# Rotary angles computed inside the first MLP, and the gMLP's v in 512-column products

## The chip, the cores and the metric

The kernel runs on one NeuronCore of one Trainium2 chip. The metric is the device time of one execution in microseconds (us), lower is better. Five engines run side by side, each with an instruction stream of its own: TensorE (PE; its weight loads are listed as PEld), VectorE (DVE), ScalarE (ACT), GpSimd (POOL) and SyncE (SP), which here issues the DMAs. An engine starts its instructions in the order of its stream; an instruction that waits holds up all that stands behind it on that engine.

## The reference

Two transformer blocks follow each other on 256 rows of 1024 columns, all in float32. The part around the change is this, cut down:

```python
# gMLP (layer 0 of the second block), GATE_DIM = 2048
z = gelu(hn @ w_in);  u, v = split(z, 2)
v = layernorm(v, ln_g, ln_b)
sv = einsum('gij,bnjgc->bnigc', masked w_s, v in blocks) + b_s
h = h + (u * sv) @ w_out
# MLP 0
h = h + square(relu(rmsnorm(h) @ w1)) @ w2
# shared latent keys and values, then attention (layer 1)
inv_freq = 10000 ** (-arange(0, 64, 2) / 64)
ang = positions[:, None] * inv_freq
c, s = cos(ang), sin(ang)          # used by apply_rope on k_pe and q_pe
```

The angles hang on the positions alone, so their sine and cosine can be made at any time before the latents.

## The kernel before, in words

**Products.** Every float32 matrix product is made in three passes: an operand is split into a high part and the rest (names ending in `h` and `l`), and `mm3` issues high times high, high times rest, rest times high. `fm` keeps the weights stationary and moves 256 columns of the activations (PE rows that read `xTh,s1h`: moving `xT`, stationary `s1`); `tm` keeps the activations stationary and moves the weights' columns (rows that read `s4h,xTh`), for one half `t` of the rows (128 of 256) at a time. `down` is `tm` with 512 columns. Every matmul has a weight load of its own.

**Weights.** All weights come as a fixed sequence of chunks (`weight_plan`), 1 MB each in two halves of 512 KB. SP loads a half into one of four `raw` buffers; ACT writes the high part of it into a slot (`s0h`, `s1h`, ...), DVE the rest (`s0l`, ...); the buffer is then loaded again. Slots are reused as soon as the chunk in them has been used up.

**Order.** The order on each engine is not written out. The kernel's parts are generators that offer one instruction at a time, and `run_threads` picks the one that an estimate of the engines' times starts first; waits such as `self.on(...)` act in that planner only. So an edit moves instructions elsewhere too.

**Stages.** Token mixer, conv FFN, gMLP, MLP 0, latents, attention, MLP 1. Between two stages stands a junction: residual, mean square on ACT, `rstd` on DVE and POOL (a power of -0.5), scaling (`r_xg`) on DVE, four transposes per 512 columns on PE, then `xTh` on ACT and `xTl` on DVE. It runs for the rows of t = 0 first; while t = 1 is in its junction, PE makes the first chunks' products for t = 0 alone ("stagger"; 4 chunks in the gMLP, `STAGV`, 3 in the MLPs, `STAG`), with `tm` and 256 columns, copied out into `tmst` and transposed. After that come `up` (w1, one chunk: 48 matmuls of 256 columns) and `down` (w2, one chunk: 24 matmuls of 512 columns) in turn; `down` i follows `up` i + 4 (`LAG`).

**gMLP v.** `v_part` multiplies one chunk of w_in (1024 rows by 256 columns, 8 row blocks) with `tm`: 24 matmuls of 256 columns for each t, 16 such products. `v_out` applies Gelu (ACT) and, after every second chunk, takes statistics of 512 columns (DVE). `layernorm` begins when all are through; the first matmul on v (`sv`) waits for it.

**Angles.** `latent_setup` runs at the start of MLP 0 and spawns `angles` with priority 8. `angles` first issues the load of `inv_freq` on SP (broadcast to 128 partitions, into a corner of `vm[0]`), converts the positions (`vm<-c_pos`), multiplies by `inv_freq`, reduces the argument and ends in two Sin activations that write `cs`. All DVE work of it writes `vm`. `cs` is first read in the latents.

Of the kernel before, what the change touches and what calls it, by code (L numbers as in the profile page):

```python
# [13 lines left out]
AF = mybir.ActivationFunctionType  # L14
# [8 lines left out]
STAG, STAGF, STAGV = 3, 4, 4  # L23
# [174 lines left out]
class Kernel:  # L198
# [611 lines left out]
    def gmlp(self, pool):  # L810
        S, V, T, G = self.S, self.V, self.T, self.G
        wsT = self.load(pool, "wsT")

        def mask_ws():
            yield self.on(("a_v", 1))
            yield from G.memset(wsT[64:, :, :64], 0.0)

        self.spawn(1, mask_ws())
        bs = self.tile(pool, [P, 8, P], "bs")
        self.bcast(bs.rearrange("p g i -> p (g i)"), "b_s")  # L820
        lng = self.bcast(self.tile(pool, [P, 2048], "lng"), "ln_g")
        lnb = self.bcast(self.tile(pool, [P, 2048], "lnb"), "ln_b")
        v = [self.tile(pool, [P, 2048], f"v{t}") for t in range(2)]
        hT = self.hT
        st = [self.tile(self.pers, [P, 4, 6], "bst", bufs=2) for t in range(2)]
        vs = []

        def v_part(w, c, t):
            o = (yield from self.bank("fm"))[:, :256]
            yield from self.tm(o, w.view(8), hT, t, range(8), ev="a_v")  # L830
            vs.append(self.spawn(1, v_out(o, c, t)))

        def v_out(o, c, t):
            yield from S.activation(v[t][:, c * 256:(c + 1) * 256], o, AF.Gelu)
            self.rel(o)
            if c % 2:
                yield from V.bn_stats(st[t][:, c // 2, :], v[t][:, (c - 1) * 256:(c + 1) * 256])

        def layernorm(t):
            yield self.join(vs)  # L840
            mv = self.tile(self.scr, [P, 2], "mv", bufs=2)
            yield from V.bn_aggr(mv, st[t])
            r = yield from self.rstd(mv[:, 1:2], 1, 1.0)
            for h in range(4):
                s = slice(512 * h, 512 * (h + 1))
                yield from V.scalar_tensor_tensor(v[t][:, s], v[t][:, s], mv[:, 0:1], lng[:, s], op0=ALU.subtract, op1=ALU.mult)
                yield from V.scalar_tensor_tensor(v[t][:, s], v[t][:, s], r, lnb[:, s], op0=ALU.mult, op1=ALU.add)
            self.set(("ln", t), v[t])

        ws = []  # L850
        for t in range(2):
            for c in range(STAGV):
                if len(ws) <= c:
                    ws.append((yield from self.chunk("a_v", c)))
                yield from v_part(ws[c], c, t)
                if t:
                    self.free(ws[c])
        for c in range(STAGV, 8):
            w = yield from self.chunk("a_v", c)
            for t in range(2):  # L860
                yield from v_part(w, c, t)
            self.free(w)
        for t in range(2):
            self.spawn(1, layernorm(t))
        self.set(("a_u", 0))
        self.set(("a_u", 1))
        aT = {}

        def block(i, o):
            u = yield from self.take(pool, [P, 512], "u", o)  # L870
            yield from S.activation(u, o, AF.Gelu)
            self.rel(o)
            sv = yield from self.bank("tp", ev=[("ln", 0), ("ln", 1)])
            for b in range(2):
                for t in range(2):
                    c0 = i * 256 + b * P
                    yield from T.matmul(sv[:, (2 * b + t) * P:(2 * b + t + 1) * P], v[t][:, c0:c0 + P], wsT[:, i, :],
                             start=True, stop=True)
            w = yield from self.take(pool, [P, 512], "svb")
            yield from V.tensor_tensor(w.rearrange("p (a i) -> p a i", a=4), sv.rearrange("p (a i) -> p a i", a=4),  # L880
                            bs[:, i:i + 1, :].to_broadcast([P, 4, P]), op=ALU.add)
            self.rel(sv)
            yield from V.tensor_tensor(w, w, u, op=ALU.mult)
            self.rel(u)
            aT[i] = yield from self.take_aT(pool, i, LAG + 1)
            yield from self.split(aT[i][0].rearrange("p a b -> p (a b)"), aT[i][1].rearrange("p a b -> p (a b)"), w)
            self.rel(w)
            self.set(("a_u", "block", i), aT[i][1])

        yield from self.updown(("a_u", "a_w_out"), 8, 1, pool, block, aT,  # L890
                               lambda t, acc: self.next_norm(t, acc, [(self.g[0], "w1_0")]), 0, ("norm_mlp_g0",))
# [479 lines left out]
            self.set(("o", t, b), l)  # L1371


    def angles(self, pool, pi):

        S, V = self.S, self.V
        scratch = self.vm[0]
        fr = self.bcast(scratch[:, 128:160], "inv_freq")
        pf = scratch[:, 160:162]
        yield from V.tensor_copy(pf, pi)  # L1380
        cs = self.cs = self.tile(pool, [P, 2, 2, 32], "cs")
        a, n = scratch[:, 0:64], scratch[:, 64:128]
        for t in range(2):
            yield from V.tensor_scalar(a[:, 32 * t:32 * t + 32], fr, pf[:, t:t + 1], None, op0=ALU.mult)
        magic = 1.5 * 2.0 ** 23
        parts = (6.28125, 0.0019340515136718750, 1.2554228305816650390625e-06)
        rest = 2 * np.pi - sum(parts)
        for big in (4096.0, 1.0):
            yield from V.tensor_scalar(n, a, float(np.float32(1.0 / (2 * np.pi * big))), magic, op0=ALU.mult, op1=ALU.add)
            yield from V.tensor_scalar(n, n, -magic, None, op0=ALU.add)  # L1390
            for c in parts + (rest,):
                yield from V.scalar_tensor_tensor(a, n, -float(np.float32(c * big)), a, op0=ALU.mult, op1=ALU.add)
        pi_lo = float(np.nextafter(np.float32(np.pi), np.float32(0)))
        yield from V.tensor_scalar(n, a, np.pi / 2, None, op0=ALU.is_gt)
        yield from V.scalar_tensor_tensor(n, n, -2 * np.pi, a, op0=ALU.mult, op1=ALU.add)
        yield from V.tensor_scalar(n, n, np.pi / 2, pi_lo, op0=ALU.add, op1=ALU.min)
        yield from V.tensor_scalar(n, n, -pi_lo, None, op0=ALU.max)
        yield from V.tensor_scalar(a, a, pi_lo, -pi_lo, op0=ALU.min, op1=ALU.max)
        yield from S.activation(cs[:, :, 0, :], n.rearrange("p (t f) -> p t f", t=2), AF.Sin)
        yield from S.activation(cs[:, :, 1, :], a.rearrange("p (t f) -> p t f", t=2), AF.Sin)  # L1400
# [16 lines left out]
    def latent_setup(self, pool):  # L1417
        self.flags = self.load(pool, "mla_flags")
        pi = self.load(pool, "pos")
        self.ckT = self.split_pair(pool, [P, 2, 2 * P], "ckT")  # L1420
        self.cqT = self.split_pair(pool, [P, 3, 2 * P], "cqT")
        self.lat_g = self.load(pool, "lat_g")
        self.vm = [self.tile(pool, [P, 1024], f"vm{t}") for t in range(2)]
        self.spawn(8, self.angles(pool, pi))
        self.gl = self.tile(pool, [P, 640], "gl")
        self.bcast(self.gl[:, 0:256], "kv_a_g")
        self.bcast(self.gl[:, 256:640], "q_g")
        self.kpT = self.tile(pool, [P, 2 * P], "kpT")
        self.pad(pool, 2 * HALF)
# [165 lines left out]
def layouts(inp):  # L1595

    a = {k: np.asarray(inp[k]) for k in inp}
    r = {}

    def cols(w, groups, ksplit=1):  # L1600
        w = w.reshape(-1, P, w.shape[-1])
        kc = w.shape[0] // ksplit
        out = []
        for g in groups:
            for s in range(ksplit):
                out.append(w[s * kc:(s + 1) * kc][:, :, g].transpose(1, 0, 2).reshape(P, -1))
        return np.ascontiguousarray(np.stack(out))

    def rows(w):
        n = w.shape[-1]  # L1610
        return np.ascontiguousarray(w.reshape(-1, 2, P, n).transpose(0, 2, 1, 3).reshape(-1, P, 2 * n))

    def run(a0, n):
        return list(range(a0, a0 + n))

    w = a["w_in"][0]
# [9 lines left out]
    w = a["w_up"][0]  # L1626
    r["w_up"] = cols(w, [run(128 * i, 128) + run(2816 + 128 * i, 128) for i in range(22)])
    r["w_down"] = rows(a["w_down"][0])
    w = a["a_w_in_2"][0]
    r["a_u"] = cols(w, [run(256 * i, 256) for i in range(8)])  # L1630
    r["a_v"] = cols(w, [run(2048 + 256 * i, 256) for i in range(8)])
    r["a_w_out"] = rows(a["a_w_out_2"][0])
    for l in range(2):
        r[f"w1_{l}"] = cols(a["mlp_w1_2"][l], [run(256 * i, 256) for i in range(16)])
# [43 lines left out]
```

## Time and profile before

| what | value |
|---|---|
| time, median of 3 runs | 956.66 us (956.59, 960.91, 956.66) |
| profiled execution | 956.88 us |
| its span (first to last instruction) | 955.1 us |
| TensorE's granted clock, mean | 0.995 |
| PE busy | 935.2 us, 98% |
| PEld / DVE / ACT / POOL busy | 90% / 68% / 54% / 3% |
| read from HBM | 165.6 MB, 174 GB/s over the span |

How to read it: the profile is one execution; its time lies 1.8 us above its span, which is what surrounds the first and the last instruction. Busy shares are means over all stages. Stages have different limits, so what an edit is worth is read from its own stretch of the span: gMLP v from about 356 to 403 us, the junction into MLP 0 and its stagger from 485 to 535 us, MLP 0's loop of `up` and `down` from 535 to 655 us, latents and attention from 680 to 770 us, the junction into MLP 1 and its stagger from 770 to 800 us.

### The profile page before, as it was taken

To read this page: it belongs to the slowest core of one execution; us is meant where nothing else is said; L and a number is where in the kernel's file an instruction comes from. 1 tells how busy PE (TensorE), PEld (TensorE's weight loads), DVE (VectorE), ACT (ScalarE), POOL (GpSimd) and SP (SyncE) were. 2 spreads that over 40 slices of the span, in tenths; PEclk is the share of its full clock that TensorE was granted. 3 is DMA by queue.
4 is the path that set the end of the run, shared out by engine and by line. 5 is a ranking of instruction groups with operands and counts; after the bars stand their busy time and mean duration, and the time that the engine had idled before them with its cause. 6 is when DMAs were issued, how large, how long until landed. Compare 5 with 4: busy or idle time off the path is not lost.

```text
span 955.1 us, 16271 instructions
## 1 busy us (share of the span) xinstructions
PE 935.2 (98%) x6531; PEld 859.5 (90%) x6531; DVE 648.8 (68%) x1031; ACT 515.1 (54%) x849; POOL 26.4 (3%) x38
## 2 busy tenths in 40 slices
PE   8999999999999999999998999999999999999997
PEld 7999878899999989999988999998889899999986
DVE  6787786889698857697556765554678677555533
ACT  5654675766566645536444644444557565544421
POOL 0001000000000001000000000000110000000000
PEclk9999999999999999999998999999999999999999
DMA  7622432746677638728545775664355377666611
GB/s 245 232 97 90 132 111 89 235 126 200 248 233 251 192 118 295 247 82 273 184 131 142 246 229 194 192 203 139 101 150 160 110 233 229 198 202 198 193 48 45
DMA packets 48749, 167.70 MB, mean 176 GB/s; under 512 B 6433, under 2 KB 7073, under 8 KB 48418
## 3 DMA queue, kind: packets, MB, share of 16 engines
q1 hardware_dynamic: 48674, 166.67, 54.8%
q8 instruction: 51, 0.84, 0.4%
q14 instruction: 24, 0.20, 0.1%
HBM read 165.60 MB, written 1.05 MB: 174 GB/s over the span
## 4 chain that ended last, share of the span: by engine, by line
PE 88%; DVE 4%; DMA 2%; ACT 2%; issue 1%; POOL 1%; SPq 1%; POOLq 0%; DVEq 0%; ACTq 0%
PE r_fm L177 46%; PE r_acc L177 37%; PE r_tp L177 5%; DMA vm<-inv_freq 1%; POOL rstd L177 1%; ACT junk L177 1%; DVE r_xg L177 1%; DMA raw<-w_v 1%; DMA raw<-w 1%; DVE s1l L177 0%; DVE xTl L177 0%; DMA raw<-w_up 0%; DVE s4l L177 0%; DVE s0l L177 0%; DVE s3l L177 0%
## 5 line engine op out<-in xcount | busy, mean ns | idle before, releaser
L177 DVE TENSOR_TENSOR s0l<-raw,s0h 128x1024 fp32r<-128x1024 f32 (+1 forms) x54 | 64.7, 1211 | 21.2 <-ACT s0h L177 21.2
L177 DVE TENSOR_TENSOR s1l<-raw,s1h 128x1024 fp32r<-128x1024 f32 (+2 forms) x54 | 64.8, 1202 | 17.3 <-ACT s1h L177 17.2
L177 DVE TENSOR_TENSOR s3l<-raw,s3h 128x1024 fp32r<-128x1024 f32 (+1 forms) x56 | 66.7, 1201 | 14.3 <-ACT s3h L177 14.2
L177 DVE TENSOR_TENSOR s2l<-raw,s2h 128x1024 fp32r<-128x1024 f32 (+1 forms) x54 | 65.1, 1212 | 16.6 <-ACT s2h L177 16.4
L177 ACT ACTIVATE s0h<-raw 128x1024 fp32r<-128x1024 f32 (+1 forms) x54 | 55.6, 1046 | 26.6 <-PE r_acc L177 17.3
L177 DVE TENSOR_TENSOR s4l<-raw,s4h 128x1024 fp32r<-128x1024 f32 (+1 forms) x46 | 55.1, 1210 | 17.4 <-ACT s4h L177 17.4
L177 PE MATMUL r_fm<-xTh,s1h 128*128 128x256 f32 x240 | 66.8, 278 | 0.0
L177 PE MATMUL r_fm<-xTh,s1l 128*128 128x256 f32 x240 | 66.7, 278 | 0.0
L177 PE MATMUL r_fm<-xTl,s1h 128*128 128x256 f32 x240 | 66.5, 277 | 0.0
L177 ACT ACTIVATE s3h<-raw 128x1024 fp32r<-128x1024 f32 (+1 forms) x56 | 57.5, 1036 | 16.4 <-PE r_acc L177 10.3
L177 ACT ACTIVATE s2h<-raw 128x1024 fp32r<-128x1024 f32 (+1 forms) x54 | 56.1, 1046 | 17.3 <-PE r_acc L177 9.8
L177 ACT ACTIVATE s1h<-raw 128x1024 fp32r<-128x1024 f32 (+2 forms) x54 | 55.9, 1038 | 15.3 <-DMA raw<-w_up 6.6
L177 DVE TENSOR_TENSOR r_q<-r_r 128x512 f32<-128x512 f32 x32 | 22.1, 691 | 57.8 <-ACT r_r L177 57.6
L177 ACT ACTIVATE s4h<-raw 128x1024 fp32r<-128x1024 f32 (+1 forms) x46 | 47.4, 1045 | 18.7 <-PE r_acc L177 10.0
L177 PE MATMUL r_fm<-xTh,s3h 128*128 128x256 f32 x200 | 55.8, 279 | 1.6 <-DVE cT L177 1.6
L177 ACT ACTIVATE r_r<-r_fm 128x512 f32<-128x512 f32 x26 | 15.5, 597 | 75.9 <-PE r_fm L177 75.9
L177 PE MATMUL r_fm<-xTl,s3h 128*128 128x256 f32 x200 | 55.6, 278 | 0.0
L177 PE MATMUL r_fm<-xTh,s3l 128*128 128x256 f32 x200 | 55.5, 278 | 0.0
L177 POOL TENSOR_TENSOR rstd<-rstd,mhalf 128x1 f32<-128x1 f32 (+1 forms) x30 | 25.5, 849 | 923.5 <-DVE rstd L177 906.8
L177 PE MATMUL r_fm<-xTh,s2h 128*128 128x256 f32 x176 | 49.0, 278 | 0.0
L177 PE MATMUL r_fm<-xTl,s2h 128*128 128x256 f32 x176 | 48.9, 278 | 0.0
L177 PE MATMUL r_fm<-xTh,s2l 128*128 128x256 f32 x176 | 48.9, 278 | 0.0
(615 smaller groups left out, 3161.2 us busy)
## 6 DMA issues: line engine op xcount, KB each, us to landing
raw<-w SPq DMA_DIRECT2D x128, 512.0 KB, 4.7
raw<-w_up SPq DMA_DIRECT2D x44, 512.0 KB, 4.8
raw<-w_down SPq DMA_DIRECT2D x22, 512.0 KB, 4.6
raw<-a_v SPq DMA_DIRECT2D x16, 512.0 KB, 5.8
raw<-a_u SPq DMA_DIRECT2D x16, 512.0 KB, 4.8
raw<-a_w_out SPq DMA_DIRECT2D x16, 512.0 KB, 4.8
raw<-w_c SPq DMA_DIRECT2D x12, 512.0 KB, 5.2
raw<-w_out SPq DMA_DIRECT2D x8, 512.0 KB, 3.7
```

The source lines that it names most:

```text
L177: f(*args, **kw)
```

## The change

Two edits that don't touch each other in the code.

1. `inv_freq` is loaded in `latent_setup`, ahead of `kv_a_g` and `q_g`, and `angles` begins with a wait of the planner for `("w1_0", "block", 4)`, the point at which the activations of MLP 0's fifth `up` (i = 4) are ready.
2. The chunks of the gMLP's v are cut the other way: 512 rows (4 row blocks) by 512 columns in place of 1024 by 256. `v_part` takes two chunks and makes one product of 24 matmuls with 512 columns; there are 8 such products. Gelu and statistics work on 512 columns each.

```diff
         def v_part(w, c, t):
-            o = (yield from self.bank("fm"))[:, :256]
-            yield from self.tm(o, w.view(8), hT, t, range(8), ev="a_v")
+
+            o = yield from self.bank("fm")
+            for i in range(2):
+                yield from self.tm(o, w[i].view(4), hT, t, range(4), k0=4 * i, first=i == 0, last=i == 1, ev="a_v")
             vs.append(self.spawn(1, v_out(o, c, t)))
 
         def v_out(o, c, t):
-            yield from S.activation(v[t][:, c * 256:(c + 1) * 256], o, AF.Gelu)
+            a = v[t][:, c * 512:(c + 1) * 512]
+            yield from S.activation(a, o, AF.Gelu)
             self.rel(o)
-            if c % 2:
-                yield from V.bn_stats(st[t][:, c // 2, :], v[t][:, (c - 1) * 256:(c + 1) * 256])
+            yield from V.bn_stats(st[t][:, c, :], a)
...
+        def pair(c):
+            w = []
+            for i in range(2):
+                w.append((yield from self.chunk("a_v", 2 * c + i)))
+            return w
+
         for t in range(2):
-            for c in range(STAGV):
+            for c in range(STAGV // 2):
                 if len(ws) <= c:
-                    ws.append((yield from self.chunk("a_v", c)))
+                    ws.append((yield from pair(c)))
                 yield from v_part(ws[c], c, t)
                 if t:
-                    self.free(ws[c])
-        for c in range(STAGV, 8):
-            w = yield from self.chunk("a_v", c)
+                    self.free(*ws[c])
+        for c in range(STAGV // 2, 4):
+            w = yield from pair(c)
             for t in range(2):
                 yield from v_part(w, c, t)
-            self.free(w)
+            self.free(*w)
...
-    def angles(self, pool, pi):
+    def angles(self, pool, pi, fr):
 
         S, V = self.S, self.V
         scratch = self.vm[0]
-        fr = self.bcast(scratch[:, 128:160], "inv_freq")
+        yield self.on(("w1_0", "block", 4))
         pf = scratch[:, 160:162]
...
-        self.spawn(8, self.angles(pool, pi))
+        fr = self.bcast(self.vm[0][:, 128:160], "inv_freq")
+        self.spawn(8, self.angles(pool, pi, fr))
...
-    r["a_v"] = cols(w, [run(2048 + 256 * i, 256) for i in range(8)])
+    r["a_v"] = cols(w, [run(2048 + 512 * i, 512) for i in range(4)], 2)
```

**Place A: the junction into MLP 0, DVE.** The rows of t = 1 are scaled here (`r_xg`) and split (`xTl`); `vm` is the scratch of the angles, `s6` a weight slot, `tmst` the copy of a staggered product.

```order
 L177 COPY tmst<-r_fm 128x256
 L177 TENSOR_SCALAR rstd<-rstd 128x1
-L177 CAST vm_5482<-c_pos 128x2
-L177 TENSOR_SCALAR vm_5482<-vm_5482 128x32
 L177 SCALAR_TENSOR_TENSOR r_xg<-x_75,rstd,gb 128x512 x2
-L177 TENSOR_SCALAR vm_5482<-vm_5482 128x32
 L177 TENSOR_TENSOR s6l<-raw,s6h 128x1024
 L177 TENSOR_TENSOR xTl<-r_tp,xTh 128x4x128
-L177 TENSOR_SCALAR vm_5482<-vm_5482 128x64 x2
-L177 SCALAR_TENSOR_TENSOR vm_5482<-vm_5482 128x64
-L177 TENSOR_TENSOR xTl<-r_tp,xTh 128x4x128
```

Twenty instructions of the angles leave this place; two of them stood between `rstd` and the `r_xg` that needs it. The second `xTl` now comes after a copy of `tmst` and one half of `s1l`.

**Place A, ACT.** After the change, from the mean square of t = 1 on (`junk`, with `ss` the sums); `r_r` is the Relu of a block.

```order
L177 ACTIVATE junk,ss<-x_75 128x512 x2
L177 ACTIVATE s6h<-raw 128x1024
L177 ACTIVATE xTh<-r_tp 128x4x128
L177 ACTIVATE s1h<-raw 128x1024
L177 ACTIVATE xTh<-r_tp 128x4x128
L177 ACTIVATE s1h<-raw 128x1024
L177 ACTIVATE s2h<-raw 128x1024
L177 ACTIVATE tmst<-r_fm 128x256
L177 ACTIVATE s2h<-raw 128x1024
L177 ACTIVATE tmst<-r_fm 128x256
L177 ACTIVATE s3h<-raw 128x1024
L177 ACTIVATE r_r<-r_tp 128x512
```

The table load and the two Sin activations, which stood behind the second `xTh` and a `tmst`, are gone from here; two copies of `tmst` now stand behind weight splits of `s2h`.

**Place B: MLP 0's loop, DVE, where the angles now stand.** `aT4l` is the last step of block 4, `r_q` the square of block 5.

```order
 L177 TENSOR_TENSOR aT4l<-r_q,r_aT4h 128x512
+L177 CAST vm_5274<-c_pos 128x2
+L177 TENSOR_SCALAR vm_5274<-vm_5274 128x32 x2
+L177 TENSOR_SCALAR vm_5274<-vm_5274 128x64 x2
+L177 SCALAR_TENSOR_TENSOR vm_5274<-vm_5274 128x64 x4
+L177 TENSOR_SCALAR vm_5274<-vm_5274 128x64 x2
+L177 SCALAR_TENSOR_TENSOR vm_5274<-vm_5274 128x64 x4
+L177 TENSOR_SCALAR vm_5274<-vm_5274 128x64
+L177 SCALAR_TENSOR_TENSOR vm_5274<-vm_5274 128x64
+L177 TENSOR_SCALAR vm_5274<-vm_5274 128x64 x3
+L177 TENSOR_TENSOR s1l<-raw,s1h 128x1024
```

All twenty stand in one run; one half of a weight split and `r_q` of block 5 follow. On ACT the table load and the two Sin stand right ahead of the Relu of block 5.

**Place C: the start of the gMLP's v, DVE.** `s2`, `s3` are slots, `bst` the statistics, `r_xg` and `xTl` the junction's rows of t = 1. After the change:

```order
L177 TENSOR_TENSOR s2l<-raw,s2h 128x1024
L177 TENSOR_TENSOR rstd<-ss 128x1
L177 TENSOR_SCALAR rstd<-rstd 128x1
L177 TENSOR_TENSOR s3l<-raw,s3h 128x1024
L177 SCALAR_TENSOR_TENSOR r_xg<-x_75,rstd,gb 128x512 x2
L177 BN_STATS bst<-v_4008 128x6
L177 TENSOR_TENSOR s3l<-raw,s3h 128x1024
L177 TENSOR_TENSOR xTl<-r_tp,xTh 128x4x128 x2
```

Before, statistics stood ahead of `rstd`, both halves of `s3l` came after `r_xg`, and the first `xTl` stood between them; now it comes behind both. On PE the transposes of t = 1 stand behind 40 matmuls of 512 columns where they stood behind 78 of 256.

## Rows read from the trace of the kernel before

**Rows 1.** The page, busy time, share of the span and instructions of each engine.

```profile
PE 935.2 (98%) x6531; PEld 859.5 (90%) x6531; DVE 648.8 (68%) x1031; ACT 515.1 (54%) x849; POOL 26.4 (3%) x38
```

**Rows 2.** Whom PE waited for: us in total, times, longest us.

```profile
PE r_tp L177 <- DVE r_xg L177: 6.6, 4, 3.8
PE r_tp L177 <- ACT tmst L177: 1.4, 2, 0.8
```

**Rows 3.** Timeline of POOL and DVE, junction into MLP 0: start, duration, [idle before].

```profile
501.98 0.55 POOL L177 TENSOR_TENSOR rstd<-rstd,mhalf 128x1 f32<-128x1 f32 x1 [12.70 <-DVE vm L177]
...
506.76 0.24 DVE L177 TENSOR_SCALAR vm<-vm 128x32 f32<-128x32 f32 x1 [4.78 <-DMA vm<-inv_freq]
506.91 1.41 DVE L177 SCALAR_TENSOR_TENSOR r_xg<-x,rstd,gb 128x512 f32<-128x512 f32 x2
```

**Rows 4.** The chain that ended last, same place: start, length, what.

```profile
499.06 7.61 DMA vm<-inv_freq
```

**Rows 5.** Timeline of PE, the stagger of MLP 0.

```profile
498.39 0.28 PE L177 MATMUL r_fm<-s3h,xTh 128*128 128x256 f32 x1
...
503.69 0.28 PE L177 MATMUL r_fm<-s4h,xTh 128*128 128x256 f32 x1
...
507.80 1.09 PE L177 MATMUL r_tp<-c_ident,r_xg 128*128 128x128 f32 x4 [3.83 <-DVE r_xg L177]
...
534.93 0.39 PE L177 MATMUL r_acc<-s2h,r_aT0h 128*128 128x512 f32 x1
```

**Rows 6.** Windows: stretch, us, busy PE, PEld, DVE, ACT, POOL, PEclk, DMA, GB/s.

```profile
504.00:506.00 2.00, 0.00 (x0) 0.00 (x0) 0.00 (x0) 0.00 (x0) 0.00 (x0) 1.00 0.84 237
508.00:510.00 2.00, 2.00 (x11) 2.00 (x11) 2.00 (x4) 0.87 (x2) 0.00 (x0) 0.50 0.09 31
512.00:514.00 2.00, 2.00 (x15) 2.00 (x15) 1.73 (x9) 0.00 (x0) 0.00 (x0) 0.77 0.27 109
```

**Rows 7.** Timeline of PE, the stagger of MLP 1, first and last.

```profile
769.51 0.28 PE L177 MATMUL r_fm<-s2h,xTh 128*128 128x256 f32 x1
...
800.54 0.39 PE L177 MATMUL r_acc<-s0h,r_aT0h 128*128 128x512 f32 x1
```

**Rows 8.** Timeline of PE: 24 `down` matmuls, then 24 of gMLP v, first and next.

```profile
344.70 0.39 PE L177 MATMUL r_acc<-s5h,r_aT1h 128*128 128x512 f32 x1
...
350.14 0.39 PE L177 MATMUL r_acc<-s2h,r_aT3h 128*128 128x512 f32 x1
...
356.52 0.28 PE L177 MATMUL r_fm<-s4h,xTh 128*128 128x256 f32 x1
...
359.35 0.28 PE L177 MATMUL r_fm<-s0h,xTh 128*128 128x256 f32 x1
```

**Rows 9.** Timeline, junction into the gMLP: DVE's first `xTl`, PE's first matmul of t = 1.

```profile
366.98 0.69 DVE L177 TENSOR_TENSOR xTl<-r_tp,xTh 128x512 fp32r<-128x512 f32 x1
...
368.71 0.28 PE L177 MATMUL r_fm<-s4h,xTh 128*128 128x256 f32 x1
```

**Rows 10.** Timeline, gMLP v: the sixth chunk (slot s4) split on DVE, then used on PE.

```profile
375.92 1.23 DVE L177 TENSOR_TENSOR s4l<-raw,s4h 128x1024 fp32r<-128x1024 f32 x1 [0.25 <-ACT s4h L177]
...
385.67 0.28 PE L177 MATMUL r_fm<-s4h,xTh 128*128 128x256 f32 x1
```

**Rows 11.** The angles by tile (count, ns min/median/max), and ACT's timeline.

```profile
L177 DVE TENSOR_SCALAR vm<-vm x10: 184/195/242, 506.8 to 515.0; 128x64 f32<-128x64 f32 x8, 128x32 f32<-128x32 f32 x2
L177 DVE SCALAR_TENSOR_TENSOR vm<-vm x9: 218/226/226, 510.6 to 514.4; 128x64 f32<-128x64 f32 x9
...
514.72 1.28 ACT L177 ACT_TABLE_LOAD   x1
516.01 0.40 ACT L177 ACTIVATE cs<-vm 128x64 f32<-128x64 f32 x2
```

**Rows 12.** Windows: MLP 0's loop; latents and attention (columns as in rows 6).

```profile
540.00:655.00 115.00, 115.00 (x782) 105.84 (x781) 66.03 (x65) 54.65 (x64) 0.00 (x0) 1.00 0.64 205
680.00:770.00 90.00, 89.13 (x555) 79.89 (x554) 66.02 (x154) 54.98 (x118) 5.12 (x6) 1.00 0.49 151
```

## The prediction

> **What bounds the kernel now.** The page comes first: PE is busy for 98% of the span [rows 1], so an edit counts only where it takes PE work out, or closes a gap in PE's stream. A busy PE is not a fast PE, so the next views are the list of PE's waits and, at the longest of them, the timelines. The list has one wait that stands out: transposes that wait for `r_xg`, 6.6 us in four waits, one of them 3.8 us long [rows 2]. The timeline puts that one into the junction of MLP 0: PE issues a matmul at 503.69 and its next instruction at 507.80 [rows 5]. POOL has the `rstd` of t = 1 at 502.53, so `r_xg` could start, but ahead of it on DVE stands a multiplication of the angles that waits 4.78 us for `inv_freq`; `r_xg` starts at 506.91 [rows 3]. The chain of waits names the load: issued at 499.06, and 7.61 us until DVE goes on [rows 4]. PE then pays a second time. Its granted clock is 1.00 up to the gap, 0.50 from 508 to 510 us (1.2 GHz in place of 2.4), and 0.77 on average from 512 to 514 [rows 6]; two levels that average 0.77 over 2 us mean 0.92 us at half, so the full clock is back at about 512.9. The other edit lies in the gMLP's v, where PE has no gap; there only the time per matmul can change.
>
> **The angles leave the junction (place A).** The gap: 507.80 - 503.69 less one matmul of 0.12 us (24 matmuls of 256 columns take 359.35 - 356.52 = 2.83 us, 0.1179 each [rows 8]) is 3.99 us. The half clock: 512.92 - 507.80 = 5.12 us at half speed lose 2.56 us. Together 6.55 us. The stagger, from its first matmul to the first `down`, takes 534.93 - 498.39 = 36.54 us [rows 5]; without both losses it would take 29.99 us, which is the best end. The other end is the stagger of MLP 1, the same code with the same order on DVE and no angles in it: 800.54 - 769.51 = 31.03 us [rows 7]. It has a wait of 0.8 us for `tmst` [rows 2], whose copy stands on ACT behind a weight split; after the change MLP 0 has the same order on ACT, so I expect most of that wait here too and take 30.85 us, near the second end: **5.7 us gained**, ends 5.5 and 6.55. Is anything else late at the transposes? With POOL's result at 502.53, `r_xg` starts at about 502.6; from its start to the transposes it was 507.80 - 506.91 = 0.89 us [rows 3, 5], which gives 503.5, and PE comes to them (now after 45 matmuls of the stagger, 498.39 + 45 x 0.1179) at 503.7. So no. On SP the `inv_freq` load passes the loads of `kv_a_g` and `q_g`, which are first used in the latents; as many small loads as before stand ahead of the next weights, so no weight load moves.
>
> **The angles in MLP 0's loop (place B).** They bring ten instructions of 0.195 us, nine of 0.226 us and a conversion on DVE, some 4.1 us in one run, and 1.28 + 0.40 us on ACT [rows 11]. I cost this at nothing. What covers it: from 540 to 655 us DVE is busy for 66.03 and ACT for 54.65 of 115 us, while PE never stops [rows 12]. Behind the run stand half a weight split, and `r_q` of block 5, whose product is used only by `down` 5, with four `up` and five `down` products of some 5.4 us ahead of it (24 matmuls of 512 columns: 350.14 - 344.70 = 5.44 us [rows 8]). ACT's Sin waits for the run, and Relu of block 5 behind it, so a PSUM bank comes free up to 4.1 + 1.7 = 5.8 us late; PE has a second bank and wants the first again two `up` products later, at least 10.9 us. If this cover were gone, up to 5.8 us would come back.
>
> **The gMLP's v (place C).** Removed: 16 products of 24 matmuls, 384 x 0.1179 = 45.28 us. Added: 8 products of 24 with 512 columns. No row before shows this product; the nearest is `down`, which also keeps activations stationary and moves 512 columns of a weight slot: 5.44 / 24 = 0.2267 us [rows 8], so 192 x 0.2267 = 43.52 us. **Gain 1.76 us.** The other end is a rate per column that stays as it is (2 x 0.1179): no gain. I take the first, as the operands' roles are those of `down`. A rule speaks against so much: the Trainium skill, "TensorE: Matmul & The Clock Gate", section "Wait — 56ns, not 53.3ns?", gives a matmul at full clock its columns over 2.4 GHz plus some 2.5 ns; an estimate from that page is 41.9 us before and 41.4 after, a gain of 0.5 us, which would put the forecast 1.3 us later. Both spacings in the trace are longer than that page's, and the narrow one by more.
>
> Against the gain: the first `xTl` of t = 1 ended at 367.67, 1.04 us before PE's first matmul of t = 1 at 368.71 [rows 9]. It now stands behind one more half split of 1.23 us [rows 10], which makes it some 0.2 us late: **-0.2 us**. The weights: of a pair of chunks the second is now wanted half a product (2.7 us) after the first, where two products (5.7 us) lay between. The sixth chunk was split by 377.15 and first used at 385.67 [rows 10]; it will be wanted about 4 us sooner, near 381.7, and still has 4.5 us to spare. The layer norm moves forward with the end of v, and PE's order puts the first `sv` eleven `up` matmuls further behind that end, which covers the longer last Gelu.
>
> **The rest.** The planner also reorders the latents and the attention. PE's idle time there is 90 - 89.13 = 0.87 us [rows 12], so I allow 0.9 us either way and expect none.
>
> **Sum.** 5.7 + 1.76 - 0.2 = 7.3 us. The profiled execution of 956.88 us would become 949.6; the median of the runs lies 0.2 us below that execution, so **949.4 us**. The best case is 6.55 + 1.76 + 0.9 = 9.2 us, 947.4; the worst within this forecast is 5.5 - 0.2 - 0.9 = 4.4 us, 952.3, with no gain from 512 columns.
>
> **The rivals.** About 0.5% (4.8 us) is what a measurement of this kernel can tell from no change: below 951.9 us is faster, above 961.4 slower.
>
> *Something else is late at the junction.* `r_xg` comes in time, but the second `xTl`, now behind a copy of `tmst` and half of `s1l`, or a `tmst` copy behind a split whose weights haven't landed, stops PE again, for 1 to 3 us, and part of the clock loss stays. Then about 3 of the 5.7 us remain, with 1.6 us of the gMLP: 952.1 us. For it: two copies now stand behind weight splits on ACT. Against: the same order in MLP 1 costs 1 us in all [rows 7]. Chance 0.12, of that 0.05 below 951.9.
>
> *The angles are paid in the loop.* If a PE product waits behind the run of place B, the 5.8 us come back: 956.66 - 7.3 + 5.8 = 955.2 us, no change. Against it stand the idle times of rows 12. Chance 0.04.
>
> *The pairs starve.* This one ends slower. A product with 512 columns can't go past its middle before the second chunk of the pair is split, and both slots come free only at the pair's end. If the second chunks of the two late pairs came later than their spare 4.5 us, PE would stop in the middle of a product, and every stop of some microseconds would cost the clock too, 2.6 us as above. To lose what the rest wins and 0.5% besides, 7.3 + 4.8 = 12.1 us, both pairs must stop for 3.5 us, so their splits must come 8 us later than now: 961.5 us and more. Against it: bytes, halves and sequence of the loads are the same. Chance 0.02.
>
> That the change doesn't do what it says is hardly open: the wait for block 4 is the planner's alone, but the order of DVE shows the angles moved.
>
> **How the numbers follow.** The forecast has 0.82, nearly all of it (0.81) below 951.9. With 0.05 of the first rival that makes 0.86 for faster; the rest of that rival, the second one and the forecast's edge make 0.12 for no change; 0.02 for slower. The range runs from the best case, 947.4, to 952.8, past the forecast's worst end and into the first rival.
>
> **What would show it.** In the profile of the changed kernel: no wait of PE for `r_xg` over 1 us, and a clock of 1.00 all through MLP 0's start; some 31 us from the first matmul of that stagger to the first `down`; 0.227 us per matmul in v, and v about 1.6 us shorter; DVE with a run of 4 us of `vm` instructions inside the loop, while PE stays full. I am wrong if PE stops for more than 1 us between 495 and 535 us, if matmuls of v take 0.236 us, or if PE shows a gap behind the Sin or in the middle of a pair.

## The result, and the profile after

The changed kernel takes 951.45 us (median of six; 950.67 to 953.41). One of the six, at a mean granted clock of 0.555, took 1562.41 us; it is in the median, which is 951.3 without it, but neither in the range nor in the ratio. The kernel before took 957.3 us (median) in the runs beside it, and the ratio is 0.9934 with a 95% interval of 0.9915 to 0.9954: about 6 us faster (4.4 to 8.1 by the interval), at the slow end of the forecast's own span (947.4 to 952.3), 2 us above its 949.4. The profiled execution after is one of 950.89 us with a span of 949.1; before it was 956.88 with 955.1.

First the page's busy times, which say little by themselves: PE has 192 matmuls fewer than in [rows 1] and is as full as it was.

```profile
PE 932.9 (98%) x6339; PEld 847.9 (89%) x6339; DVE 649.3 (68%) x1033; ACT 511.9 (54%) x839; POOL 26.2 (3%) x38
```

The list of PE's waits (us in total, times, longest) answers to [rows 2]: the wait of 3.8 us for `r_xg` is gone, and the copies of `tmst` cost about what they did, in more and shorter waits.

```profile
PE r_tp L177 <- DVE r_xg L177: 2.7, 3, 1.5
...
PE r_tp L177 <- ACT tmst L177: 1.1, 4, 0.5
```

The timeline of PE from the stagger of MLP 0 to its first `down`, which answers to [rows 5]. The transposes of `r_xg` start at 501.56, with no idle time in brackets; the only idle time left is that of the `tmst` transposes.

```profile
496.26 0.28 PE L177 MATMUL r_fm<-s3h,xTh 128*128 128x256 f32 x1
...
501.56 0.60 PE L177 MATMUL r_tp<-c_ident,r_xg 128*128 128x128 f32 x4
...
509.74 0.55 PE L177 MATMUL r_tp<-c_ident,tmst 128*128 128x128 f32 x3 [0.18 <-ACT tmst L177]
...
514.36 0.55 PE L177 MATMUL r_tp<-c_ident,tmst 128*128 128x128 f32 x3 [0.20 <-ACT tmst L177]
...
527.32 0.39 PE L177 MATMUL r_acc<-s2h,r_aT0h 128*128 128x512 f32 x1
```

The timeline of DVE for the same stretch, against [rows 3]: `r_xg` starts as soon as POOL has its `rstd`, and the angles stand 30 us further on, in the loop.

```profile
500.43 1.42 DVE L177 SCALAR_TENSOR_TENSOR r_xg<-x,rstd,gb 128x512 f32<-128x512 f32 x2 [0.66 <-POOL rstd L177]
...
530.90 0.16 DVE L177 CAST vm<-c_pos 128x2 f32<-128x2 int32 x1
531.09 0.85 DVE L177 TENSOR_SCALAR vm<-vm 128x32 f32<-128x32 f32 x4
...
535.00 0.53 DVE L177 TENSOR_SCALAR vm<-vm 128x64 f32<-128x64 f32 x3
```

Windows of the kernel after, with the columns of [rows 6]. The granted clock stays at 1.00, the 2.4 GHz level, where it fell to 0.50 before. The last window is the latents and the attention: 87.96 us, of which PE is idle for 1.54.

```profile
504.00:506.00 2.00, 2.00 (x20) 2.00 (x19) 1.64 (x2) 0.40 (x2) 0.00 (x0) 1.00 0.92 366
508.00:510.00 2.00, 1.82 (x15) 1.55 (x14) 1.92 (x3) 2.00 (x5) 0.00 (x0) 1.00 0.68 166
512.00:514.00 2.00, 2.00 (x19) 1.94 (x17) 0.98 (x2) 1.54 (x3) 0.00 (x0) 1.00 0.79 279
...
675.63:763.59 87.96, 86.42 (x536) 76.63 (x534) 65.18 (x153) 51.77 (x112) 4.85 (x6) 1.00 0.48 144
```

The same stretch of the kernel before took 86.26 us, with 0.87 idle.

```profile
683.25:769.51 86.26, 85.39 (x535) 76.74 (x534) 63.51 (x151) 53.18 (x114) 5.12 (x6) 1.00 0.48 147
```

Where the 6.0 us of the two profiled executions come from is read best by cutting both spans at the same matmuls on PE: the first of v, the first `up` of the gMLP, the first of each stagger, the first `down` of each MLP, the first of the latents. All stage times of this document are made so, in us, each from one profiled execution. A stage begins where PE issues its first matmul.

```
stage                     before   after   difference
mixer                     169.11  168.60   -0.51   (code unchanged)
FFN                       187.41  187.12   -0.29   (code unchanged)
gMLP v                     46.10   44.86   -1.24
gMLP, the rest             95.77   95.68   -0.09
MLP 0, stagger             36.54   31.06   -5.48
MLP 0, loop               148.32  148.31   -0.01
latents and attention      86.26   87.96   +1.70
MLP 1, stagger             31.03   30.91   -0.12
MLP 1, loop to the end    154.56  154.60   +0.04
```

So the junction gave its 5.5 us, v gave 1.2, and the attention took 1.7 back. The first two lines are the same code and vary from execution to execution (the changed kernel's mixer alone took 172.98 us in another profile), so 0.8 of the 6.0 us is not the change's.

### The profile page after: what moved, and what is told of

It reads as the page before. It is cut to its first block, busy times and chain, and to the rows that moved or that the text cites. A ratio compares the mean times of both kernels' runs of the same rounds, so it can differ in the third digit from the quotient of the medians.

```text
span 949.1 us, 15879 instructions
## 1 busy us (share of the span) xinstructions
PE 932.9 (98%) x6339; PEld 847.9 (89%) x6339; DVE 649.3 (68%) x1033; ACT 511.9 (54%) x839; POOL 26.2 (3%) x38
## 4 chain that ended last, share of the span: by engine, by line
PE 88%; DVE 5%; ACT 3%; DMA 2%; issue 1%; POOL 1%; POOLq 0%; ACTq 0%; DVEq 0%
PE r_fm L177 45%; PE r_acc L177 38%; PE r_tp L177 5%; DMA raw<-w 2%; ACT junk L177 1%; DVE s1l L177 1%; POOL rstd L177 1%; DVE r_xg L177 1%; DVE s0l L177 0%; DMA raw<-w_up 0%; DVE s3l L177 0%; ACT p L177 0%; DVE s4l L177 0%; DVE xTl L177 0%; DVE r_cv L177 0%
```

## The experiments

Twelve runs followed, ten of them of new kernels and two of kernels that had run, each beside the kernel before. Ratios carry 95% intervals; with a width of some 0.4%, about 4 us, they can't resolve single terms, so the stage times carry the argument.

**The angles alone, and the new v alone.** The first kernel has the diff's parts in `angles` and `latent_setup`, the second its parts in the gMLP and in the weight layout.

> The kernel before with the edit of the angles alone. If the two edits are worth what their own stretches show, the stagger of MLP 0 (first matmul to first down) takes 31.1 us as in the changed kernel, against 36.5 before, at a granted clock of 1.00, and the gMLP's v stays at 46.1 us; from before's 956.9 us that is 951.4, give or take what the planner's new order does to the latents and the attention (up to 1.7 us, as the changed kernel shows). If the gain of the junction needed the other edit, the stagger stays above 33 us.

Measured: 953.94 us, ratio 0.9970 (0.9951 to 0.9989). The stagger of MLP 0 took 31.50 us, the loop 148.32, v 46.11, the latents and attention 87.81.

> The kernel before with the edit of the gMLP's v alone. By its own stretch: v takes 44.9 us against 46.1, the stagger of MLP 0 stays at 36.5 us with its gap and its half clock, and the time is 955.6 us, give or take 1.7 us for the latents and the attention. A rival, that the shorter v is given back at the next wait (the load of inv_freq lands when it lands), would show a gap in MLP 0 that is longer by 1.2 us and a time of 956.9 us.

Measured: 956.58 us, ratio 1.0004 (0.9984 to 1.0025), which doesn't tell a gain of 1.2 us from none. The stages do: v 44.87 us, the stagger 36.28, the loop 148.32, the attention 86.25. With the angles left where they were, the old gap stands again in the waits of this kernel (its longest is the one in MLP 0's junction):

```profile
PE r_tp L177 <- DVE r_xg L177: 6.1, 4, 3.6
```

What follows: the parts add. The angles bring the 5 us of the junction, and the loss in the attention (1.55 us here, 1.70 in the kernel after) comes with them too, though that code lies 150 us further on. The v edit gives 1.23 us in its own stage and changes no other stage by more than 0.3 us, the two of unchanged code ahead of it aside.

**The load's wait, or the angles' operations?** The row of `inv_freq` is loaded in the gMLP, and the twenty operations stay in the junction, in front of and between the halves of MLP 0's first work.

```
-        fr = self.bcast(scratch[:, 128:160], "inv_freq")      (in angles)
+        self.fr = self.bcast(self.tile(self.pers, [P, 32], "fr"), "inv_freq")   (in gmlp, behind lnb)
```

> The kernel before, but inv_freq is loaded in the gMLP, some 140 us ahead, into a tile of its own; the twenty DVE instructions of the angles stay in the junction of MLP 0. Theory: the wait for the load made the gap, so r_xg is late only by a conversion and a multiplication, 0.4 us, PE's gap before the transposes is under 0.6 us, the clock stays at 1.00 and the stagger takes 31 to 32 us, the time 951.5 to 952.5 us. Rival: the 4.1 us of DVE work in the junction cost by themselves (xTl comes late behind them); then the stagger takes 33.5 us or more and PE waits for xTl.

Measured: 958.78 us, ratio 1.0022 (1.0004 to 1.0041). The stagger fell to 31.22 us, so the wait on the load was nearly the whole of the junction's loss (PE still waits 0.7 us for `r_xg`). But the whole missed its 951.5 to 952.5 us: the loop took 151.03 us in place of 148.32, the end of the kernel 156.70 in place of 154.56, and the gMLP behind v 96.47 in place of 95.77. In the loop, `up` products of the slots s6 and s1 had a pitch of 0.118 us per matmul where they had 0.114. The new tile had moved others, so two more kernels separate the load from the places. One puts the row where an unused gap was, so that every other tile keeps its address; the other adds only the 128 bytes.

```
-        self.pad(self.consts, 2 * HALF)
+        self.fr = self.tile(self.consts, [P, 2 * HALF], "fr")     (and the load in gmlp)
```

> The load of inv_freq early, in the gMLP, into a place that was an unused gap, so that every other tile keeps the address it had before; the angles' operations stay in the junction. Theory (the wait on the load is the junction's loss; the slower matmuls of the first such experiment came from moved addresses): MLP 0's first stage 31.2 us, its loop 148.3, FFN and rest as before, the latents and attention 86.3 (order kept) to 87.9 (order changed); the whole 951 to 953.5. Rival (the early load itself, or DVE's operations, slow the loop): loop 151 again and the whole 956 to 959.

Measured: 951.76 us, ratio 0.9938 (0.9917 to 0.9959). The stagger took 31.02 us, the loop 148.33, the end 154.56, the attention 86.23, v 46.11. On DVE's timeline the angles now stand in the junction around `r_xg`. Their arithmetic doesn't hold it up; their conversion waits 1.02 us for another small load, the positions, so `rstd` comes late, `r_xg` starts 4.78 us after the stage's first matmul where it was 4.17 in the kernel after, and PE waits 0.21 us for it:

```profile
502.35 0.17 DVE L177 CAST vm<-c_pos 128x2 f32<-128x2 int32 x1 [1.02 <-DMA c_pos<-pos]
...
502.89 0.38 DVE L177 TENSOR_SCALAR vm<-fr,vm 128x32 f32<-128x32 f32 x2
503.30 0.20 DVE L177 TENSOR_SCALAR vm<-vm 128x64 f32<-128x64 f32 x1
503.71 1.41 DVE L177 SCALAR_TENSOR_TENSOR r_xg<-x,rstd,gb 128x512 f32<-128x512 f32 x2 [0.21 <-POOL rstd L177]
504.60 0.63 PE L177 MATMUL r_tp<-c_ident,r_xg 128*128 128x128 f32 x4 [0.21 <-DVE r_xg L177]
```

The other one:

```
+        self.pad(self.pers, 2 * HALF)      (in gmlp, behind lnb)
```

> The kernel before with 128 unused bytes per partition among the lasting tiles, which puts every tile behind them, xT and the later weight slots among them, where the first early-load experiment had them; no instruction added or taken away. Theory (place alone changes the matmuls' pitch): the junction's first stage stays 36.5 us, MLP 0's loop takes 151.0 in place of 148.3, the rest 156.7 in place of 154.6; the whole 960 to 963. Rival (the pitch came from the load or the order): loop 148.3, the whole 956.7.

Measured: 965.75 us, ratio 1.0091 (1.0064 to 1.0118), the loop 151.03 us, the end 156.72, the gMLP behind v 96.47: within 0.02 us these three stages of the first try. The expectation was wrong in three details. The median lies above its 963; the stagger took 35.38 us, not 36.5, with a gap of 3.6 us still in it; and by the order in which the kernel opens its pools xT and the slots s0 to s3 don't move, while the slots s4 to s7 and the stages' own tiles do. The rows, first of the kernel before and then of this one, show the 48 `up` matmuls of slot s6 from their first row to the `down` behind: 5.46 us, and 5.65.

```profile
551.31 0.29 PE L177 MATMUL r_fm<-xTh,s6h 128*128 128x256 f32 x1
...
556.77 0.39 PE L177 MATMUL r_acc<-s0h,r_aT2h 128*128 128x512 f32 x1
```

```profile
551.73 0.28 PE L177 MATMUL r_fm<-xTh,s6h 128*128 128x256 f32 x1
...
557.38 0.40 PE L177 MATMUL r_acc<-s0h,r_aT2h 128*128 128x512 f32 x1
```

What follows: in the junction the waits for small loads cost, the row's above all, and not the angles' arithmetic; and 128 bytes in the wrong place cost this kernel more (5.6 us in these three stages) than the v edit gains. Of that kernel's median, 8 us over its neighbours, the profile of its fastest execution (961.69 us) shows some 4 to 5; the rest was not traced.

**Is the loop's room real?** The kernel after, but with the load asked for only behind block 4, so that its time on the queues lies in the loop too.

```
     yield self.on(("w1_0", "block", 4))
+    fr = self.bcast(scratch[:, 128:160], "inv_freq")      (and no load in latent_setup)
```

> The kernel after, but the load of inv_freq is asked for only behind block 4 of MLP 0, so that its 7.6 us on the queues and the angles' twenty operations all lie in the loop. Theory (loop has room for both): MLP 0's loop stays at 148.3 us and its first stage at 31.1 (within 0.5), the whole within 0.3% of the kernel after (948.6 to 954.3). Rival (angles were free only because their row was there early; with the load in the loop the chunk loads behind it come late): the loop is longer by 1 to 7.6 us.

Measured: 953.18 us, ratio 0.9949 (0.9928 to 0.9969); the loop 148.28 us, the stagger 31.71. The angles ran on DVE from 540 us on, cut in two by the work of a block, and the window of that stretch has PE busy throughout at full clock:

```profile
535.00:550.00 15.00, 15.00 (x100) 13.66 (x100) 11.46 (x29) 8.12 (x11) 0.00 (x0) 1.00 0.47 137
```

The cover held for the load as for the arithmetic. The 1.7 us by which its median exceeds that of the kernel after are within the spread of both, and the intervals of the two ratios overlap.

**What slows the attention.** The kernel after, in which from the latents to the end of the attention the planner no longer chooses: it takes the threads, and the engine of each copy, in the order that the kernel before chose.

```
+        if self.picks:
+            born = self.picks.popleft()
+            pick = next(th for th in self.threads if th[1] == born)
...
-        if self.est.free["ACT"] <= self.est.free["DVE"]:
+        if self.copies.popleft() if self.copies else self.est.free["ACT"] <= self.est.free["DVE"]:
```

> The changed kernel, but from the latents to the end of the attention the instructions are issued in the order of the kernel before (the planner's picks and its choices of ACT or DVE for copies are replayed from a table). Theory: the 1.7 us that this stretch took longer come from the planner's new order alone, so it takes 86.3 us again (88.0 in the changed kernel), and the time is 949.2 us against 950.9. Rival: they come from what the shift of all that stands ahead does to the loads or the engines there; then it stays near 88 us.

Measured: 951.41 us, ratio 0.9937 (0.9912 to 0.9962); latents and attention 86.24 us, the other stages as after. So the loss is the new order and nothing else. The medians don't show it: 949.2 us was expected, and 951.41 can't be told from the 951.45 of the kernel after. The chain of work that ended last shows what the order does. After the change it runs through DVE and ACT, where splits of weights (`s0h`, `s0l`, `s2h`, `s2l`; ACT 0.95 us, DVE 1.23 each) stand between the steps of a softmax (`sm`, `p`):

```profile
732.61 1.29 ACT p L177 x5
733.90 0.95 ACT s0h L177
734.86 0.02 issue
734.88 1.23 DVE s0l L177
736.10 0.34 DVE oTl L177
736.44 0.61 DVE sm L177
...
738.63 0.95 ACT s2h L177
739.58 0.02 issue
739.60 1.23 DVE s2l L177
740.83 0.61 DVE sm L177
```

On PE's timeline the softmax's result `p` comes late in that stretch. These are two of four such steps:

```profile
733.60 1.16 PE L177 MATMUL r_tp<-p,vm 128*128 128x128 f32 x8 [0.27 <-ACT p L177]
...
743.48 0.94 PE L177 MATMUL r_tp<-c_ident,p 128*128 128x128 f32 x4 [0.23 <-DVE p L177]
```

From the matmul ahead to the four it takes 0.64, 0.50, 0.62 and 0.37 us, where with the old order no step to an operation on `p` takes more than 0.27. That is some 1.4 of the 1.70 us. PE's idle time grew by 0.67 us alone (1.54 against 0.87): a row of 512 columns counts as busy for 0.39 us and the next can follow after 0.23, so the first part of a stop doesn't show as idle.

With the old order put back, the same stretch of the chain has PE alone in it:

```profile
730.08 1.34 PE r_tp L177 x12
731.42 0.47 PE r_fm L177 x4
731.89 2.92 PE r_acc L177 x16
734.82 0.44 PE r_tp L177 x4
735.26 1.09 PE r_acc L177 x6
736.34 0.89 PE r_tp L177 x8
```

All fourteen profiles, before and after among them, fall into two groups by this: 87.75 to 88.04 us with the angles in the loop, whatever v is, and 86.2 to 86.4 with the angles in the junction or with the old order put back.

**What gives the gain in v.** The half-row chunks in pairs as in the change, but products of 256 columns:

```
-            for i in range(2):
-                yield from self.tm(o, w[i].view(4), hT, t, range(4), k0=4 * i, first=i == 0, last=i == 1, ev="a_v")
+            for h in (0, 256):
+                for i in range(2):
+                    yield from self.tm(o[:, h:h + 256], w[i].view(4), hT, t, range(4), k0=4 * i, c0=h, n=256, ...)
```

> The kernel after with its half-row chunks taken in pairs, but every product of gMLP's v again 256 columns wide (384 matmuls in place of 192). Theory (the width alone gives the gain): v takes 46.1 us as before, 1.2 more than after's 44.86, junction 31.1 and attention 88.0 as after; the whole 952.7. Rival (the chunks' layout or the fewer waits give it): v stays at 44.9.

Measured: 952.73 us, ratio 0.9963 (0.9945 to 0.9981); v 44.79 us. The theory fell: the gain is there with all 384 matmuls. (That the whole met the theory's 952.7 us is chance.) Their pitch was 0.1177 us, as before, up to the transposes of the second row tile in the middle of the stage, and 0.1133 from there to the end. Chance, or the order? The same kernel again:

> The kernel with pairs of half-row chunks and products of 256 columns once more, unchanged. In its first profile the pitch in v was 0.1177 us until the pause of the transposes for t = 1 and 0.1133 behind it, v 44.79 us in all. Theory A (this layout and order give the shorter pitch): the same again, v 44.8. Theory B (the pitch has two levels, and which one follows a pause is chance, execution by execution): the pitch may stay at 0.1177 and v then takes 46.0.

Measured: v 44.80 us, with the pitches as in the first profile, group by group; 953.1 us in the one execution. So hardly chance. The next kernel goes back to the chunks of before (256 columns, all rows) and keeps only the bank that two products share, with its one eviction of 512 columns:

```
-                yield from self.tm(o, w[i].view(4), hT, t, range(4), k0=4 * i, first=i == 0, last=i == 1, ev="a_v")
+                yield from self.tm(o[:, i * 256:(i + 1) * 256], w[i].view(8), hT, t, range(8), ev="a_v")
...
-    r["a_v"] = cols(w, [run(2048 + 512 * i, 512) for i in range(4)], 2)
+    r["a_v"] = cols(w, [run(2048 + 256 * i, 256) for i in range(8)])
```

> The kernel after with v's weights cut as before (256 columns, all rows in a chunk), two such chunks into the halves of one bank and one eviction of 512 columns for both: products of 256 columns as in the pairs of half-row chunks, but each with one chunk. Theory A (the half-row chunks' places, h behind h at twice the stride, give the shorter pitch seen there): pitch 0.1177 us throughout, v 46.0. Theory B (the shared bank and half as many evictions, or the pause they leave, give it): 0.1133 us behind the pause for t = 1, v 44.8. Either way the first stage of MLP 0 is 31 to 32 and the attention 88 as after.

Measured: 954.72 us, ratio 0.9955 (0.9930 to 0.9980); v 44.79 us. The layout of the chunks does nothing either. The first product behind the transposes, 24 matmuls from its first row to the next product's, takes 2.72 us here, where it took 2.82 before (368.71 [rows 9] to 371.53).

```profile
370.62 0.28 PE L177 MATMUL r_fm<-s4h,xTh 128*128 128x256 f32 x1
...
373.34 0.28 PE L177 MATMUL r_fm<-s0h,xTh 128*128 128x256 f32 x1
```

In these three runs the stage behind v gave part of it back: it took 96.13 to 96.14 us in place of 95.68, because its first `up` products now had the pitch of 0.118. Against before, v and the rest of the gMLP together win 0.95 us with 256 columns and 1.3 us with 512.

**The early row and the new v together.** The early row in the old gap, and the v of the change; no wait for a block, and the planner left alone.

> The kernel before with v in products of 512 columns as in the change, and the load of inv_freq early into the unused gap; the angles' operations stay in the junction, so that the copies of the attention keep the order of before. Theory (the attention's loss came with the angles moved into the loop): v 44.9 us, MLP 0's first stage 31.0, its loop 148.3, latents and attention 86.3, which is 1.7 us under the kernel after: 949.7 us where that measures 951.4. Rival (the new v changes the planner's order there as well): attention 87.9, the whole as the kernel after.

> The kernel after once more, unchanged, on the chip of the version that may beat it: ratio to before 0.9934 as measured (within 0.002), v 44.86 us, latents and attention 87.96, first stage of MLP 0 31.1 to 31.5. Stages with the same code that differ from the first profile show what one execution alone can't be trusted with: the mixer and the FFN by up to 3 us, the others by under 0.5.

Measured on the same chip: 949.93 us for the new version (ratio 0.9915, 0.9890 to 0.9940), 951.99 for the kernel after (0.9933, 0.9910 to 0.9957). v took 44.86 us in both, the stagger of MLP 0 30.78 and 31.00, the latents and attention 86.25 and 88.04. The medians differ by 2.1 us and the intervals overlap; the 1.8 us of the attention are plain in the stages. The second profile of the kernel after also shows how far one execution can be trusted: its stages agree with the first within 0.1 us, but the mixer, the same code in all kernels, took 172.98 us against 168.60. The two profiles of the pairs of 256 columns differ by more: 31.18 and 32.06 us in the stagger of MLP 0, 31.56 and 30.35 in that of MLP 1, so a difference of under 1 us in a stagger tells nothing.

## Why the prediction came out as it did

**Place A, the junction: right.** Forecast 5.7 us and a stagger of 30.85, measured 5.48 and 31.06. The text had PE at the transposes "after 45 matmuls of the stagger"; with the stagger's new start that is 496.26 + 45 x 0.1179 = 501.57, and the row stands at 501.56. In this profile nothing else was late there, and the clock never fell; of the wait of 0.8 us for `tmst` that was taken over from MLP 1, 0.4 us came, in two gaps of 0.2. That the load's wait was the cause, and not the twenty operations, is shown by the early row in the old gap (31.02 us).

**Place B, the loop: right.** Forecast nothing, measured -0.01 us; the run of 4.6 us on DVE, with the load inside the loop as well, left PE full.

**Place C, v: the sign right, the reason wrong.** The step that failed is "192 x 0.2267 = 43.52 us", with the pitch of `down` taken for the new product. The kernel after shows 0.2287 us: the 24 matmuls between the rows below take 5.49.

```profile
355.72 0.39 PE L177 MATMUL r_fm<-s4h,xTh 128*128 128x512 f32 x1
...
361.21 0.39 PE L177 MATMUL r_fm<-s1h,xTh 128*128 128x512 f32 x1
```

That makes 43.9 us and a gain of 1.3 to 1.4 in the products, as far as rows of two decimals tell; 1.24 of it arrived, and the stage's other 0.9 us, its transposes, stayed. The feared 0.2 us of a late `xTl` did not come: the first product of the second row tile has the same pitch. The page's estimate of 0.5 us for the gain (the Trainium skill, "TensorE: Matmul & The Clock Gate", section "Wait — 56ns, not 53.3ns?") fell short of the 1.24. The text set it aside because the narrow spacing in the trace was longer than the page's "by more"; that holds as a share (8% against 5%), not in time (8.7 ns a matmul against 10.9). But the deeper reason was not the width. At the short one of its two pitches, 384 x 0.1133 = 43.5 us, the narrow product is no slower than the wide one; the kernel before just ran all of v at the long pitch. The new v wins because 512 columns took 0.229 us throughout, and a shared bank with narrow products wins nearly as much.

**The attention: the mis-sized term.** The text said "I allow 0.9 us either way and expect none", by PE's idle time of 0.87 us in that stretch. It measured +1.70, and that, with 0.3 less from v and 0.2 less from the junction, makes 2.2 us, against 2.05 from 949.4 to 951.45. That the sum closes so well is partly luck, as stages of unchanged code differ by more from one execution to the next. It is partly luck, too, that the time stayed inside the forecast's span: this term went past its 0.9 us, and the span's slow end had room for that because it counted no gain from v. The bound was taken the wrong way round: idle time bounds what a better order can give back, not what a worse one can cost. DVE was busy for 63.5 and ACT for 53.2 of the 86.3 us there, and their work lies between dependent steps of the softmax, so a weight split in the wrong place makes `p` late and PE waits for it.

**The rivals.** *Something else late at the junction* lands near the measured time (952.1 us), but of its 1 to 3 us the two profiles of the kernel after have 0.4 and 0.5, with the clock at 1.00, so it isn't what held the time at 951.45. It is real all the same. In all eight profiles with the angles in the loop PE waits for `tmst` in MLP 0's stagger, 0.4 to 1.5 us, and in the second run of the pairs of 256 columns it is what the rival describes: a split whose weights land late, the copy of `tmst` behind it, and PE behind the copy.

```profile
510.43 1.06 ACT L177 ACTIVATE s2h<-raw 128x1024 fp32r<-128x1024 f32 x1 [1.78 <-DMA raw<-w]
511.39 0.36 ACT L177 ACTIVATE tmst<-r_fm 128x256 f32<-128x256 f32 x1
...
511.81 0.38 PE L177 MATMUL r_fm<-s4h,xTh 128*128 128x256 f32 x1 [1.46 <-ACT tmst L177]
```

There the stagger took 32.06 us, and the granted clock stayed at 1.00. In the three profiles with the row early and the angles in the junction no such wait is listed (staggers of 30.78 to 31.22 us); whether the order on ACT makes that difference was not tested. *The angles paid in the loop* and *the pairs starve* did not happen.

## What to carry to other kernels

A load that the first operation of a thread waits for blocks everything queued behind it on that engine: ask for it a stage earlier and leave the arithmetic alone, which here won as much as moving the arithmetic and kept the order of later stages. Its other loads want the same care: the positions, still waited for, made PE stand for 0.2 and 0.7 us in two profiles. Where a planner sets the order by its own account of time, an edit in one stage reorders others; compare the order of every stage whose engines feed dependent steps, and price a reorder by the operations that can slip in between dependent steps (here splits of 0.95 and 1.23 us), not by the idle time that is there. Before a wider product is credited to its width, run the narrow product with the rest of the edit.

## What the runs showed of the chip that was not expected

Back-to-back matmuls of 256 columns run at one of two pitches at the full granted clock, 0.1133 to 0.1138 or 0.1175 to 0.1179 us. Inside a stage with one address per operand the pitch changes only where transposes or a pause come between, and then holds for dozens of products; in the staggers the same code had either pitch in different executions, while in v it came out alike every time (long in all five profiles with narrow products in banks of their own, short behind the transposes in all three with a shared bank). Moving the later weight slots and the tiles behind them by 128 bytes set the long pitch for the `up` products of s6 and s1 in MLP 0's loop, of which only s6 had moved, and of s4 in MLP 1's, where s1 kept the short one. What chooses the pitch is not settled: the kind of matmul behind the transposes doesn't, and no run took bank, eviction and pause apart, nor the place of the transposes: in v five matmuls stand between their two groups where the long pitch followed, ten where the short one did. Products of 512 columns in v showed one pitch, 0.2283 to 0.2292 us, in all six profiles that have them.
